# Add + RMSNorm streamed over one core: residual loads moved from SyncE's DMA queue to ScalarE's

## Chip, cores, metric

One core of a Trainium2 chip runs the kernel. The metric is the device time of one execution in microseconds (us).

## The reference

```python
x, residual: [32, 2048, 2048] float32;  gamma: [2048] float32;  eps = 1e-6
z = x + residual
rms = np.sqrt(np.mean(z ** 2, axis=-1, keepdims=True) + eps)
return (z / rms * gamma).astype(np.float32)
```

65536 rows of 8 KB. Two tensors are read and one is written, 1610.6 MB in all, with three or four simple operations per element.

## The kernel before

Rows go through SBUF (the on-chip memory) in tiles of 7 rows per partition: 128 partitions x 56 KB = 7168 KB per transfer. The first two tiles have 3 and 5 rows. Per tile there are three transfers (x in, residual in, z out) and this compute:

- VectorE adds the residual to z in place, in two parts, "a" of 3 rows and "b" of 4 rows.
- ScalarE squares each row with a running sum, part a then part b, and takes the root of each part.
- VectorE takes the reciprocals and scales each row by it and by gamma.

There are two z buffers, and one residual area of 11 rows for tiles of 7, so that the next residual tile may be loaded once part a of the add has freed its rows. SyncE issues every transfer, in this order (shortened, comments added):

```python
    def load_r(sp, t, d=0):
        i = t.i + d
        e = entry(i)
        inc(
            sp.dma_start(out=r_area[:, e : e + sizes[i], :], in_=rows(r_f, i)),
            "r_in",
            i,
        )

    def sp_turn(sp, t):
        i = t.i
        t.wait(sp, "done", -1)              # tile i-1 is scaled
        inc(sp.dma_start(out=rows(o_f, i - 1), in_=z[(i - 1) % 2][...]), "s_out", i - 1)
        if i == last:
            return
        t.wait(sp, "add_a")                 # part a of tile i is added: rows free
        load_r(sp, t, 1)
        t.wait(sp, "s_out", -1)             # store of tile i-1 has landed: z buffer free
        # ... last tile: x in four parts ...
        load_x(sp, t, 1)
```

ScalarE's turn for one tile (a `chain.wait` between its own instructions keeps their order):

```python
    def act_turn(s, t, chain):
        i, p = t.i, t.p
        for h, (a, b) in enumerate(parts(i)):
            chain.wait()
            t.wait(s, "add_a" if h == 0 else "add_b")
            inc(
                act_part(s, chain, z[p], a, b, ssq[p][h], rms[p][h][:, : b - a]),
                "rms_a" if h == 0 else "rms_b",
                i,
            )
```

## Time and profile before

| | before |
|---|---|
| time, median of 3 runs | 3726.41 us (3726.31 to 3726.53) |
| bytes moved, rate on the plateau | 1610.7 MB, 434 GB/s |
| share of the 16 DMA engines that is busy | 99.9% |
| VectorE, ScalarE busy | 62%, 29% |
| one tile | 50.77 us |

The lines behind this table are shown in the prediction. How to read them: in the queue lines the last number is the time that the queue's packets took as a share of 16 engines over the whole span; in the issue lines the last number is the median time from the issue to the landing, waiting in the queue included; in the instructions in order of time, the bracket is the time for which the engine sat idle and what ended it. As in the prediction, T is the moment at which VectorE starts to add a tile, which is when its x has landed.

### The profile page before, as it was taken

The numbers are of one execution on the slowest core, as the hardware profiler recorded it, in microseconds if no ns is written. First come the engines' busy times: TensorE is split into PE (matmuls) and PEld (weight loads), VectorE is DVE, ScalarE is ACT, GpSimd is POOL, SyncE is SP. The second block draws the span as 40 slices with busy tenths as digits, with TensorE's granted clock in tenths as the row PEclk, the third lists the DMA queues.
The fourth block names the chain that finished last, engine by engine and source line by source line (L and its number), as shares of the span: only waits on it lengthen the run. The fifth ranks groups of instructions, "written<-read, shape, count | busy, mean of one in ns | idle before, by whom it ended". The sixth has DMA issues, their size and how long they took to land.

```text
span 3724.5 us, 3677 instructions
## 1 busy us (share of the span) xinstructions
DVE 2302.6 (62%) x816; ACT 1072.4 (29%) x1176; POOL 0.2 (0%) x4
## 2 busy tenths in 40 slices
DVE  5666665566665566665566665566665566655566
ACT  2233322233322233322233322233322233322233
POOL 0000000000000000000000000000000000000000
DMA  9999999999999999999999999999999999999999
GB/s 421 431 434 434 433 434 436 434 434 434 434 434 434 434 434 434 434 434 434 434 434 434 434 434 434 434 434 434 434 434 434 434 434 434 434 434 434 434 433 399
DMA packets 32964, 1610.69 MB, mean 432 GB/s; under 512 B 3712, under 2 KB 3776, under 8 KB 3776
## 3 DMA queue, kind: packets, MB, share of 16 engines
q1 hardware_dynamic: 32960, 1610.66, 99.9%
q14 instruction: 4, 0.03, 0.0%
HBM read 1073.77 MB, written 536.87 MB: 432 GB/s over the span
## 4 chain that ended last, share of the span: by engine, by line
DMA 66%; DVE 22%; issue 10%; ACT 1%; SPq 0%; DVEq 0%; ACTq 0%
DMA out_dram<-z 33%; DMA z<-in_x_dram 33%; DVE z L170 15%; DVE z L175 7%; ACT sq_junk L221 1%; DMA r_area<-in_gamma_dram 0%; ACT rms L229 0%; DVE rstd L195 0%; DVEq L126 0%; SPq L255 0%; DVE r_area L271 0%; ACTq L209 0%; ACTq L126 0%; DVE tail_rstd L288 0%; SPq L160 0%
## 5 line engine op out<-in xcount | busy, mean ns | idle before, releaser
L170 DVE TENSOR_TENSOR z<-z,r_area 128x8192 f32<-128x8192 f32 (+2 forms) x150 | 1109.5, 7437 | 1253.0 <-DMA z<-in_x_dram 1226.8
L221 ACT ACTIVATE sq_junk<-z 128x2048 f32<-128x2048 f32 x512 | 963.4, 1882 | 2617.9 <-DVE z L170 2606.5
L175 DVE SCALAR_TENSOR_TENSOR z<-z,rstd,gamma_tile 128x2048 f32<-128x2048 f32 x505 | 1153.5, 2344 | 5.2
L195 DVE RECIPROCAL rstd<-rms 128x4 f32<-128x4 f32 (+2 forms) x146 | 25.3, 174 | 130.8 <-ACT rms L229 130.8
L221 ACT ACTIVATION_READ_ACCUMULATOR sq_junk<-z 128x1 f32 x512 | 95.4, 186 | 0.0
L229 ACT ACTIVATE rms<-ssq,eps_tile 128x4 f32<-128x4 f32 (+2 forms) x146 | 43.3, 297 | 13.4
L175 DVE SCALAR_TENSOR_TENSOR z<-z,tail_rstd,gamma_tile 128x2048 f32<-128x2048 f32 x7 | 16.2, 2346 | 0.1
L273 DVE LOAD_MASK_SELECT gamma_tile<-r_area x1 | 0.0, 14 | 16.4 <-DMA r_area<-in_gamma_dram 16.4
L273 DVE STREAM_SHUFFLE gamma_tile<-r_area 128x2048 f32<-128x2048 f32 x1 | 2.3, 2290 | 0.0
L271 DVE MEMSET r_area<- 128x2048 f32 x1 | 1.8, 1765 | 0.4 <-issue 0.4
L221 ACT ACT_TABLE_LOAD x1 | 1.3, 1283 | 0.9 <-SPq L75 0.9
L229 ACT ACT_TABLE_LOAD x1 | 1.3, 1283 | 0.1
L229 ACT ACTIVATE tail_rms<-tail_ssq,eps_tile 128x2 f32<-128x2 f32 (+1 forms) x4 | 1.2, 295 | 0.1
L270 DVE MEMSET eps_tile<- 128x1 f32 x1 | 0.1, 59 | 1.0 <-SPq L75 1.0
L288 DVE RECIPROCAL tail_rstd<-tail_rms 128x2 f32<-128x2 f32 (+1 forms) x4 | 0.6, 158 | 0.0
L345 POOL MEMSET const-bfloat16-1.0<- 128x1 bf16 x1 | 0.1, 102 | 0.0
L345 POOL MEMSET const-uint8-127<- 128x1 uint8 x1 | 0.1, 102 | 0.0
L345 POOL MEMSET const-float32-1.0<- 128x1 f32 x1 | 0.1, 99 | 0.0
L345 POOL MEMSET const-float32-0.0<- 128x1 f32 x1 | 0.1, 98 | 0.2 <-issue 0.2
## 6 DMA issues: line engine op xcount, KB each, us to landing
r_area<-in_residual_dram SPq DMA_DIRECT2D x72, 7168.0 KB, 27.2
z<-in_x_dram SPq DMA_DIRECT2D x71, 7168.0 KB, 33.8
out_dram<-z SPq DMA_DIRECT2D x71, 7168.0 KB, 34.4
z<-in_x_dram SPq DMA_DIRECT2D x3, 2048.0 KB, 26.3
out_dram<-z SPq DMA_DIRECT2D x3, 2048.0 KB, 14.1
r_area<-in_residual_dram SPq DMA_DIRECT2D x1, 5120.0 KB, 25.3
z<-in_x_dram SPq DMA_DIRECT2D x1, 5120.0 KB, 36.8
out_dram<-z SPq DMA_DIRECT2D x1, 5120.0 KB, 24.8
```

The source lines that it names most:

```text
L170: return v.tensor_add(out=s, in0=s, in1=r_area[:, e + a : e + b, :])
L175: ins = v.scalar_tensor_tensor(out=s, in0=s, scalar=rs[:, c + g - a : c + g - a + 1], in1=gamma_tile[:, :], op0=mult, op1=mult,)
L195: v.reciprocal(out=rstd[p][h][:, :n], in_=rms[p][h][:, :n]).then_inc(dve, U)
L221: s.activation(out=sq_junk[:, :], in_=src[:, g, :], func=Act.Square, accum_out=sq[:, g - a : g - a + 1],)
L229: return s.activation(out=rm, in_=sq[:, : b - a], func=Act.Sqrt, bias=eps_tile[:, :], scale=inv_d)
L270: v.memset(eps_tile[:, :], float(eps))
L271: v.memset(stage, 0.0).then_inc(tail_ev["add"], 1)
L273: v.stream_shuffle(gamma_tile[:, :].rearrange("p (a b) -> p a b", a=16), stage, [0] * 32)
L288: v.reciprocal(out=tail_rstd[:, a:b], in_=tail_rms[:, a:b]).then_inc(dve, U)
L345: nc = _bacc.Bacc("TRN2", target_bir_lowering=False, num_devices=1)
```

## The change

The intent: a residual load can be issued the moment its rows are free, by the engine that is waiting for that very event anyway, while SyncE keeps only the stores and the x loads. The core of the diff:

```diff
+    r_full = r_f[starts[2] :, :].rearrange("(n p r) m -> n p r m", p=P, r=R)
...
         inc(
-            sp.dma_start(out=r_area[:, e : e + sizes[i], :], in_=rows(r_f, i)),
+            sp.dma_start(
+                out=r_area[:, e : e + sizes[i], :],
+                in_=rows(r_f, i) if t.it is None else r_full[t.it + (i - 2)],
+            ),
...
         if i == last:
             return
-        t.wait(sp, "add_a")
-        load_r(sp, t, 1)
         t.wait(sp, "s_out", -1)
...
             t.wait(s, "add_a" if h == 0 else "add_b")
+            if h == 0 and i > 0:
+                load_r(s, t, 1)
             inc(
...
-        with s.Fori(0, 2 * n_iter, 2) as it:
+        with s.Fori(0, 2 * (n_iter - 1), 2) as it:
...
-        chain.n = n + 2 * R * n_iter
-        for i in range(HI, last):
+        chain.n = n + 2 * R * (n_iter - 1)
+        for i in range(HI - 2, last):
```

An unused semaphore (`fin`) goes as well. ScalarE's loop addresses the residual by its loop register, and its last iteration is peeled (written out after the loop).

More of the change, by code (lines that the diff above doesn't have):

```diff
@@ L96 @@
     s_tail = sem("s_tail")
-    fin = sem("fin")
     tail_ev = {k: sem(f"tail_{k}") for k in ("add", "rms", "done")}
```

## The prediction

> **What bounds the kernel now.** I read the head of the page and its DMA lines first, then the issues with their landing times, then one period of the instructions in order of time, then the waits of the issuing queue, then the two ends of the run. Head, slices and queues:
>
> ```profile
> span 3724.5 us, 3677 instructions
> DVE 2302.6 (62%) x816; ACT 1072.4 (29%) x1176; POOL 0.2 (0%) x4
> ...
> DMA  9999999999999999999999999999999999999999
> GB/s 421 431 434 434 433 434 436 434 434 434 434 434 434 434 434 434 434 434 434 434 434 434 434 434 434 434 434 434 434 434 434 434 434 434 434 434 434 434 433 399
> ...
> q1 hardware_dynamic: 32960, 1610.66, 99.9%
> ```
>
> One queue fills all 16 engines for 99.9% of the span. At the plateau of 434 GB/s its 1610.66 MB need 1610.66 / 0.434 = 3711 us; the span is 3724.5. So everything outside the plateau, both ends together, is about 13 us (0.35%). VectorE, the busiest compute engine, has 38% of the span free.
>
> ```profile
> r_area<-in_residual_dram SPq DMA_DIRECT2D x72, 7168.0 KB, 27.2
> z<-in_x_dram SPq DMA_DIRECT2D x71, 7168.0 KB, 33.8
> out_dram<-z SPq DMA_DIRECT2D x71, 7168.0 KB, 34.4
> ```
>
> A transfer of 7168 KB (7.34 MB) takes 7.34 / 0.434 = 16.9 us alone; every kind needs 27 to 34 us from issue to landing, so each waits 10 to 17 us behind another. Three of them make a tile: 3 x 16.9 = 50.8 us. One tile by the instructions in order of time (start, duration, engine, what):
>
> ```profile
> 1808.80 15.16 DVE L170 TENSOR_TENSOR z<-z,r_area 128x6144 f32<-128x6144 f32 x2 [17.58 <-DMA z<-in_x_dram]
> 1815.38 0.33 SPq L140 DMA_DIRECT2D r_area<-in_residual_dram  x1
> ...
> 1824.05 1.88 ACT L221 ACTIVATE sq_junk<-z 128x2048 f32<-128x2048 f32 x1 [2.20 <-DVE z L170]
> ...
> 1825.69 0.33 SPq L134 DMA_DIRECT2D z<-in_x_dram  x1
> ...
> 1842.01 0.34 SPq L149 DMA_DIRECT2D out_dram<-z  x1
> 1859.57 15.16 DVE L170 TENSOR_TENSOR z<-z,r_area 128x6144 f32<-128x6144 f32 x2 [17.59 <-DMA z<-in_x_dram]
> ```
>
> The period is 1859.57 - 1808.80 = 50.77 us, which is the three transfers and nothing else. Call 1808.8, when x of this tile is in, T. The store before has been in the queue since about T-17 and lands at T+16.9; the residual load is issued at T+6.6, the x load at T+16.9, the next store at T+33.2, each while an earlier transfer is still moving. The compute chain from x landed to the next store issued is 33.2 us of 50.8, so 17.6 us of it are slack: VectorE then idles (the 17.58) for the next x.
>
> ```profile
> SPq L140 <- DVE z L170: 1689.1, 72, 24.5
> SPq L149 <- DVE z L175: 1191.7, 73, 32.5
> SPq L134 <- DMA out_dram<-z: 697.1, 71, 10.0
> ```
>
> These are SyncE's waits as issuer. The first looks like the target: 1689.1 us behind the add before a residual load. But the add is what frees the rows; ScalarE waits for the same event. The store wait after it takes 697.1 / 71 = 9.8 us more, so the x load is never held by the add.
>
> [...] The trace agrees so far as it can: an issue is 0.33 us and lies beside a full pipe. [...] It does show that arrivals are in order of issue and that the steps from store to load to load cost nothing visible (50.77 against 3 x 16.9).
>
> **The change, part by part.**
>
> Removed: SyncE's wait for the add and its residual issue, for 72 tiles (tiles 0 and 1 stay on SyncE). That frees 72 x 0.33 = 24 us of SyncE, an engine that waits nearly always: 0 us on the path.
>
> Added: 72 issues on ScalarE, directly after the add that frees the rows and before the first square. The order of instructions shows, in the loop, one more register instruction ahead of each; VectorE's instructions are unchanged. At 0.33 to 0.6 us each (0.33 is SyncE's median, 0.58 its longest) this is 24 to 43 us of ScalarE. ScalarE's first group of squares ends and then it sits 2.20 us waiting for the second add (the bracket at 1824.05), so the issue is absorbed there and the second group starts when it did. On the path: 0 us. The loop loses one iteration of two tiles, which are peeled: same work.
>
> Moved: the moment of the residual issue does not move. Before, it is at T+6.6, right behind the add; after, the add's event lets ScalarE issue at T+6.6. What moves is its place. Before, it queues behind the store. After, it shares the engines with it. [...] The engines were never empty, so x lands when it does now[...]. The next store is issued at T+33.2, before x lands. The period stays 50.8.
>
> Ends: [...] the stores of the tile before still fill the engines until about 3706, and the last x part arrives when it did. Estimate 0 to 2 us. At the start the x load of tile 2 waits for the store of tile 0 (50.72) and not for the add (45.6), so nothing is won. Sum: 3726 + 0 to 2 us.
>
> **The rivals.** First, a bubble: x is issued only when the store before has wholly landed, and the store now lands late. If the residual gets more than its share, it may be through before x starts, and the engines stand idle for about 2 us per tile: 72 x 2 = 144 us, 3870 us (+4%). [...] For it: the 16 engines are not level (the DMA share in the last 18.5 us is only 0.63)[...].
>
> Second, a price of interleaving: store packets (SBUF to HBM) alternate with load packets of 56 KB. Per engine a transfer is 8 packets of 2.1 us; some 16 switches per tile. To cost 2%, a switch must cost 1.03 us / 16 = 64 ns. The queue of before changes direction twice per tile without a visible cost. [...]
>
> Third, a gain: mixed directions could run above the plateau. [...] a separate queue can otherwise win only the ends, 13 us: 3713 at the very best.
>
> Fourth, no interleaving at all: each engine finishes a transfer before it changes rows. Then the order is that of before, and the time too.
>
> **Range and chances.** The centre is the time before, 3726. Below it lie the ends (13 us, hardly reachable), above it the switch price and small bubbles. Range 3717 to 3742. Faster by over 2% would need 446 GB/s or more: 0.02. Slower by over 2% needs the bubble or 64 ns a switch: 0.05. Within 2%: 0.93.
>
> **What would show it.** A second hardware queue with about 72 x 7.34 = 528 MB, a third of the bytes, and the first with 1082 MB; together still 99% or more, slices at 434. Landing times: store 34.4 to about 43, x 33.8 to about 25, residual 27.2 to about 34; if they stay at 34, 34 and 27, there was no interleaving, and the time is right for another reason. SyncE's wait for the store should take over nearly all the 1689 us that it spent on the add. VectorE's wait for x stays near 17.6 us per tile, and the wait of the second reciprocal stays at 1.7. Wrong, and how: [...] DMA slices below 9 or a share near 96% mean the bubble; x landing before the residual, with VectorE waiting on the residual, means that the shares are not equal.

Passages are cut from the prediction at the marks. The cut sum under "Moved" assumed equal shares of an engine for two queues (later runs showed that their packets alternate one by one while both have work) and a start time of a load that no trace showed. It put the store's landing at T+25.7, the residual's at T+40.4 and x's at T+50.7, hence the period of 50.8 us; the landing times of 43, 25 and 34 us further down come from it. The "0 to 2 us" for the ends came from a first tail add that slips from 3677.2 to about 3679. The whole came to 3726 + 0 to 2 us, and the range of 3717 to 3742 also covered the cut allowance.

## The result, and the profile after

| | before | after |
|---|---|---|
| median of 4 runs | 3726.43 us | 3725.11 us |
| lowest to highest | 3726.31 to 3726.53 | 3724.70 to 3725.53 |

Ratio 0.9996, 95% interval 0.9979 to 1.0014: the same. (A ratio here is the mean time of one kernel's fast runs over the mean of the other's fast runs of the same rounds, so it need not equal the ratio of the medians.)

Head, slices and queues of the kernel after:

```profile
span 3723.7 us, 3798 instructions
...
GB/s 421 431 434 435 434 434 435 434 435 435 434 434 434 434 434 434 434 434 433 434 434 434 434 434 434 434 434 434 434 434 434 434 434 434 434 434 434 434 432 398
...
q1 hardware_dynamic: 22592, 1082.17, 67.2%
q10 hardware_dynamic: 10368, 528.49, 32.8%
```

The second queue carries the predicted 528 MB, the two together 100%, and the plateau stands at the same 434 GB/s. The issues, from the page's last part, show that the order did change:

```profile
r_area<-in_residual_dram ACTq DMA_DIRECT2D x72, 7168.0 KB, 35.5
z<-in_x_dram SPq DMA_DIRECT2D x71, 7168.0 KB, 27.5
out_dram<-z SPq DMA_DIRECT2D x71, 7168.0 KB, 40.8
```

The residual takes 8 us longer than before and the store 6 us longer, since they share the engines (packets of 2.116 us of the two queues alternate on an engine while both have work); the x load takes 6 us less, because it is issued later. One tile in order of time:

```profile
1807.81 15.16 DVE L172 TENSOR_TENSOR z<-z,r_area 128x6144 f32<-128x6144 f32 x2 [17.64 <-DMA z<-in_x_dram]
1814.55 0.34 ACTq L141 DMA_DIRECT2D r_area<-in_residual_dram  x1
...
1823.07 1.88 ACT L223 ACTIVATE sq_junk<-z 128x2048 f32<-128x2048 f32 x1 [1.67 <-DVE z L172]
...
1831.02 0.33 SPq L135 DMA_DIRECT2D z<-in_x_dram  x1
...
1841.03 0.34 SPq L153 DMA_DIRECT2D out_dram<-z  x1
1858.63 15.16 DVE L172 TENSOR_TENSOR z<-z,r_area 128x6144 f32<-128x6144 f32 x2 [17.63 <-DMA z<-in_x_dram]
```

The residual is still issued at T+6.7 and the next store at T+33.2. The x load is now issued at T+23.2, 6.3 us later than before, and yet the next tile starts 50.8 us after this one, as before. ScalarE's slack ahead of its second group went from 2.20 to 1.67 us: the issue was paid from there. SyncE's waits:

```profile
SPq L135 <- DMA out_dram<-z: 2828.4, 71, 43.0
SPq L153 <- DVE z L177: 735.1, 73, 32.2
```

Before, in the lines shown in the prediction, SyncE waited 1689.1 us for adds, 1191.7 for scaled tiles and 697.1 for stores, 3577.9 together; in these two lines it now waits 3563.5. A wait of 1689 us was removed from an engine, and it waits as long as it did.

### The profile page after: what moved, and what is told of

Its sections match the earlier page's. It is cut to its first block, busy times and chain, and to the rows that moved or that the text cites. A ratio compares the mean times of both kernels' runs of the same rounds, so it can differ in the third digit from the quotient of the medians.

```text
span 3723.7 us, 3798 instructions
## 1 busy us (share of the span) xinstructions
DVE 2302.6 (62%) x816; ACT 1072.4 (29%) x1176; POOL 0.2 (0%) x4
## 4 chain that ended last, share of the span: by engine, by line
DMA 67%; DVE 22%; issue 9%; ACT 2%; SPq 0%; DVEq 0%; ACTq 0%
DMA out_dram<-z 39%; DMA z<-in_x_dram 27%; DVE z L172 15%; DVE z L177 7%; ACT sq_junk L223 1%; ACT rms L231 0%; DVE rstd L197 0%; SPq L259 0%; DVEq L127 0%; DVE r_area L275 0%; ACTq L211 0%; ACTq L127 0%; SPq L141 0%; DVE tail_rstd L292 0%; SPq L162 0%
## 6 DMA issues: line engine op xcount, KB each, us to landing
r_area<-in_residual_dram ACTq DMA_DIRECT2D x72, 7168.0 KB, 35.5
z<-in_x_dram SPq DMA_DIRECT2D x71, 7168.0 KB, 27.5
out_dram<-z SPq DMA_DIRECT2D x71, 7168.0 KB, 40.8
```

## The experiments

All results are correct to the reference.

For some readings I summed the packet records of the traces myself. In these records each of the 16 engines moves a transfer of 7168 KB as 8 packets of 56 KB, followed by a packet of 4 bytes. "Long" is said of a packet that takes clearly more than the usual 2.116 us. The profile's views do not print such sums, so the tables of them are in ordinary fences. Columns of the first: the mean period of a tile; the mean time of one 56 KB packet on either queue (the median is 2.116 us in every run); the share of packets over 2.2 us on either; and the time per tile and engine in which no packet ran, which is the period minus 24 packets (16 of them on SyncE's queue where there are two queues, all 24 where there is one).

```
run          period   packet us          over 2.2 us      idle, us
             us       SyncE   ScalarE    SyncE  ScalarE   per tile
before       50.80    2.118   -          0.1%   -          0.0
after        50.80    2.118   2.117      0.0%   0.1%       0.0
x_first      54.55    2.193   -          8.3%   -          1.9
late_r_mid   52.44    2.185   2.182      6.7%   10.6%      0.0
late_r_end   54.61    2.158   2.268      6.1%   13.6%      1.9
late_r_sq1   50.81    2.118   2.117      0.2%   0.1%       0.0
late_r_sq2   50.86    2.120   2.122      1.1%   2.0%       0.0
dve_1        50.80    2.118   2.117      0.1%   0.1%       0.0
dve_2        51.80    2.140   2.184      3.1%   10.1%      0.1
```

The theory: the engines are kept full by both kernels, and while they are, the order of packets does not matter. The rivals: a small real gain or price of the second queue (a price per switch), or a compute chain that carries part of the time.

**after_again: the changed kernel, five rounds.** No edit.

> The changed kernel once more, for a narrower interval. Theory (the engines are always full, only the order of packets changes): 3725 us, ratio to before between 0.999 and 1.001. Rival (a small real gain or price of the second queue): a ratio that stays away from 1 by over 0.1% in every round.

Measured: 3724.97 us median, 3724.78 to 3725.36, against 3726.38; ratio 0.9996 (0.9983 to 1.001). No run of before lies below 3726.0 and none of after above 3725.6, so some 1.4 us (0.04%) may well be real, but the interval includes 1. I did not find its place for certain: in the two profiles the kernel after is already 0.3 us ahead at the first add, before any changed instruction has run. It stays open.

**x_first: the kernel before, x ahead of the residual on the one queue.**

```diff
-        t.wait(sp, "add_a")
-        load_r(sp, t, 1)
         t.wait(sp, "s_out", -1)
         load_x(sp, t, 1)
+        t.wait(sp, "add_a")
+        load_r(sp, t, 1)
```

> The kernel before, all on SyncE's queue, with the x load ahead of the residual load (it still waits for the store before; the residual load still waits for its rows). The bytes are the same. Theory: what keeps the engines full while the store's landing is reported and the x load starts up is the residual transfer in the pipe; without it there is one empty gap of 1.5 to 2 us per tile, 72 x 1.5 to 2 = 108 to 144 us, so 3830 to 3870 us; the DMA rate falls from 434 to about 418 to 422 GB/s. Rival (order never matters, as the bytes alone set the time): 3726 us within 8.

Measured: 4000.99 us, ratio 1.0739 (1.0722 to 1.0755). The queue line and one tile:

```profile
q1 hardware_dynamic: 32960, 1610.66, 96.4%
```

```profile
1939.79 15.16 DVE L170 TENSOR_TENSOR z<-z,r_area 128x6144 f32<-128x6144 f32 x2 [21.38 <-DMA r_area<-in_residual_dram]
...
1956.60 0.33 SPq L134 DMA_DIRECT2D z<-in_x_dram  x1
1956.97 0.43 SPq L140 DMA_DIRECT2D r_area<-in_residual_dram  x1
```

The store lands at T+16.8, the x load is issued then, and nothing else is in the pipe. So order does matter where it lets the pipe run dry: the rival that bytes alone set the time is out. The gap was foreseen (1.9 us per tile in the table, 1.5 to 2 expected), but the price is twice that: 54.55 - 50.80 = 3.75 us. The other 1.8 us are in packets that take longer than 2.116 us. In each tile they come in two sets, one per engine each time: the first x packet after the gap, at T+17.8, takes about 2.8 us, and the last residual packet before the next store, at T+50.3, about 3.3 us (means of the tiles in the middle of the run).

**late_r_mid: the changed kernel, residual issued after the first group of squares.**

```diff
             t.wait(s, "add_a" if h == 0 else "add_b")
-            if h == 0 and i > 0:
-                load_r(s, t, 1)
             inc(act_part(...), "rms_a" if h == 0 else "rms_b", i)
+            if h == 0 and i > 0:
+                load_r(s, t, 1)
```

> The changed kernel with the residual load issued on ScalarE after the first group of squares, about 6.5 us later (T+13.2 in place of T+6.7, T being when x is in). Theory: it is still issued before the store would land by itself at T+16.9, so the engines stay full: 3725 us within 8. Landing times move towards: residual about 31, x about 31, store about 37 us. Rival (the early issue is what the changed kernel lives on, or ScalarE's issue delays the squares): slower by 0.5% or more.

Measured: 3847.26 us, ratio 1.0329 (1.0313 to 1.0345). I had expected no change: this is the one clear miss. The queues and a tile by the windows (period, busy times, clock, DMA share, GB/s):

```profile
q1 hardware_dynamic: 22592, 1082.17, 67.0%
q10 hardware_dynamic: 10368, 528.49, 32.7%
```

```profile
1921.45 15.16 DVE L172 TENSOR_TENSOR z<-z,r_area 128x6144 f32<-128x6144 f32 x2 [19.01 <-DMA z<-in_x_dram]
1934.36 0.34 ACTq L141 DMA_DIRECT2D r_area<-in_residual_dram  x1
...
1940.37 0.33 SPq L135 DMA_DIRECT2D z<-in_x_dram  x1
```

```profile
1921.45:1973.75 52.30, 31.42 (x12) 14.61 (x16) 0.00 (x0) 1.00 1.00 421
```

The engines are busy for 99.7% and move only 421 GB/s: the busy share shows no loss, and the rate does. The loss sits in long packets: the first residual packets at T+13.9 to T+14.5 on 12 of the 16 engines (in a tile from the middle of the run), and again one packet per engine around T+46. Those 12 engines had just finished the store. I had reckoned with the store's landing at T+16.9, but that is the slowest engine. In the kernel before, the 16 parts of one transfer land over 4.0 us (median; in a transfer from the middle 10 engines lie within 0.4 us, and the last five come 2.6 to 4.0 us after the first), so the first part of the store lands at about T+12.9. In late_r_mid it lands at T+14.2 (median), 1.3 us after the residual is issued.

The engines hardly stand idle over this: 0.07 us per tile and engine, at T+13 to T+15. The time is in the packets, and how long the first residual packet on an engine takes goes with how soon after the issue it starts:

```
starts, us after the issue    0.9-1.1  1.1-1.3  1.3-1.5  1.5-1.8  1.8-2.4  2.4-2.8  2.8-3.2  3.2-3.6
us above 2.116, mean          0.80     0.70     0.55     0.39     0.29     0.28     0.11     0.02
```

The first x packets of x_first, on engines that did stand idle, give the same: 0.84 us more at 0.9 to 1.0 us after the issue, 0.54 at 1.2 to 1.5. So this set goes with the lead, the time from the issue to the moment when an engine gets to the load (below about 3 us the first packet is long), and not with whether the engine is empty. The set around T+46 is not explained by this, since those packets had been queued for long.

**late_r_end: the same after both groups.**

```diff
+            if h == 1 and i > 0:
+                load_r(s, t, 1)
```

> The changed kernel with the residual load issued on ScalarE after both groups of squares, at about T+24. Theory: the store then lands at T+16.9 with nothing else in the pipe, so each tile has a gap of at least 1.5 to 2 us, and the late residual shares with the x load and with the next store and lands after x: at least 3830 us, probably 3850 to 4050, and VectorE waits for the residual in place of x. Rival (the moment of the issue does not matter while the bytes are the same): 3725 us.

Measured: 4019.76 us, ratio 1.079 (1.0773 to 1.0806), inside the range. (The residual is issued at T+23.6.) The wait of VectorE turned over to the residual, as expected:

```profile
DVE z L172 <- DMA r_area<-in_residual_dram: 1547.1, 72, 26.4
```

The table shows the two parts again, 1.9 us of idle engines and 1.8 us of long packets per tile (54.61 - 50.80 = 3.81, rounded parts). "As soon as its rows are free" is thus worth 7.9% in the kernel after; but the kernel before had that issue time already.

**late_r_sq1 and late_r_sq2: between the changed kernel and late_r_mid.** The issue follows the first, or the second, square of the first group.

```diff
             for g in range(a, b):
                 ... square of row g ...
+                if then is not None and g - a + 1 == min(N, b - a):   # N = 1 or 2
+                    then()                                              # load_r(s, t, 1)
```

> The changed kernel with the residual load issued on ScalarE after the first square, about 2.1 us later than in the changed kernel (T+8.8). Theory, corrected after the run with 6.2 us of delay cost 122 us: the 16 engines are up to 4 us apart, the leading ones finish the store at about T+12.9, and the residual's first packet comes about 1 us after its issue; so nothing runs dry: 3725 us within 8. Rival (the loss grows evenly with the delay, 122 us per 6.2 us): about 3766 us.

> The same with the issue after the second square, about 4.1 us later (T+10.9). Theory: first packet at about T+12, just ahead of the leading engines' end of the store at T+12.9: 3725 to 3760 us, and hardly any packet longer than 2.2 us. Rival (even growth): about 3806 us.

Measured: 3724.99 us (ratio 0.9996) and 3727.12 us (1.0001, interval 0.9984 to 1.0018; 3725.85 to 3730.72). The first says nothing: its issue is no later than in the kernel after (1915.93 - 1909.18 = T+6.75), because ScalarE issues the transfer while the square is still running:

```profile
1909.18 15.16 DVE L172 TENSOR_TENSOR z<-z,r_area 128x6144 f32<-128x6144 f32 x2 [17.64 <-DMA z<-in_x_dram]
1915.77 1.88 ACT L223 ACTIVATE sq_junk<-z 128x2048 f32<-128x2048 f32 x1 [33.67 <-DVE z L172]
1915.93 0.34 ACTq L141 DMA_DIRECT2D r_area<-in_residual_dram  x1
```

The second is at T+8.8, two and not four us later:

```profile
1913.69 15.16 DVE L172 TENSOR_TENSOR z<-z,r_area 128x6144 f32<-128x6144 f32 x2 [17.57 <-DMA z<-in_x_dram]
1922.47 0.34 ACTq L141 DMA_DIRECT2D r_area<-in_residual_dram  x1
```

An even growth of the loss (122 us for 6.2 us of delay) would make 40 us of these 2.0 us of delay; measured are 2 against the kernel after. So the loss does not grow evenly: it sets in steeply between T+8.8 and T+12.9. That fits the lead of about 3 us: in late_r_sq2 the first part of the store lands at T+11.9 (median), 3.1 us after the residual is issued, and 1 to 2% of the packets are already long.

**before_8k and after_8k: seven times as many packets.** Rows dealt to the partitions so that a partition's rows are not contiguous in DRAM, in both kernels.

```diff
-        return t[starts[i] : starts[i] + P * k, :].rearrange("(p r) m -> p r m", r=k)
+        return t[starts[i] : starts[i] + P * k, :].rearrange("(r p) m -> p r m", r=k)
```

> The kernel before with rows dealt to partitions so that a partition's rows lie 128 rows apart in DRAM: each packet becomes 8 KB in place of 56 KB, seven times as many, same bytes and result. It is the base for the next run; its own time is open, 3726 to 3900 us.

> The changed kernel with the same 8 KB packets, so about 112 changes of queue per tile and engine in place of 16. Theory (a change of queue costs nothing): the same as the run with 8 KB packets on one queue, within 0.5%; and with finer packets the landing times come nearer to the equal-share sum of the prediction, store 43, x 25, residual 34 us, if the difference of the changed kernel from it (40.8, 27.5, 35.5) comes from whole 2.1 us packets. Rival (a switch costs 20 ns or more): slower than its base by 112 x 0.02 = 2.2 us per tile, 4% or more.

Measured: 3798.37 us (1.0193 of before; 1.0176 to 1.021, "unclear" against a bound of 2%) and 3791.67 us (1.0175). Two queues are 0.18% faster than one here (3791.67 / 3798.37 = 0.9982). In before_8k a tile takes 51.80 us (one in the middle, 1895.99 to 1947.79), and its 22.02 MB make 425 GB/s in place of 434; the order of addresses changed with the packets, so their size alone is not shown to be the cause. The number of changes of queue was not the expected 112. Joining each packet record to the one that ends as it begins, I count about 54 per tile and engine, and about 7 in the kernel after (not 16): while both queues have work they alternate packet by packet, and for the rest of the tile one queue has the engine alone. The rival of a price per switch is still out: 20 ns would have cost 54 x 0.02 = 1.1 us per tile, 2%. After:

```profile
r_area<-in_residual_dram ACTq DMA_DIRECT2D x72, 7168.0 KB, 34.7
z<-in_x_dram SPq DMA_DIRECT2D x71, 7168.0 KB, 28.2
out_dram<-z SPq DMA_DIRECT2D x71, 7168.0 KB, 41.9
```

Against 35.5, 27.5 and 40.8 with large packets, the residual and the store moved only a little towards the 34 and 43 of the prediction, and the x load away from its 25. So whole packets are not the main reason for that difference. By the packet records, the first residual packet in the kernel after starts 3.9 us after its issue and every engine has one by 5.6 us; with 8 KB packets 3.5 to 3.9 us. On engines with nothing to do it was 0.95 us, which is 0.62 us after the end of the issue (the x load of x_first).

**dve_1 and dve_2: a longer compute chain in the kernel after.** One or two sums over four rows before the scaling, result unused.

```diff
             v.wait_ge(dve, own(i, h))
+            for j, _ in enumerate((4,) if h == 0 and i > 1 else ()):      # dve_2: (4, 4)
+                v.reduce_sum(out=junk[:, 2*p+j : 2*p+j+1], in_=z[p][:, <rows of part b>, :] ..., axis=X)
```

> The changed kernel with one more VectorE operation per tile between the adds and the scaling, a sum over four rows (8192 elements, about 8.6 us as the add of that size), result unused. It also covers the 1.7 us wait for the second root, so the store is issued about 7 us later, at T+40. Theory (the compute chain is hidden while the store is queued before the engines run out of x): 3725 us within 8, VectorE's wait for x down from 17.6 to about 10.7 us per tile. Rival (the chain carries part of the time): up to 72 x 7 = 500 us more.

> The same with two such sums, about 17.2 us, so the store is issued at about T+48.7, 2 us before x is in at T+50.7. Theory with the spread of the engines (the leading ones are through with x up to 4 us earlier, at about T+46.8, and a first packet comes 1 us after its issue): part of the engines run dry each tile, and packets around it get longer: 1 to 3 us per tile, 3790 to 3940 us. Rival (only the slowest engine counts; the slack of 17.6 us still covers it): 3725 us within 8.

Measured: 3724.78 us (0.9996) and 3803.35 us, ratio 1.0209 (1.0192 to 1.0226: slower, though "unclear" against a bound of 2%). In dve_1, VectorE does 604 us more and nothing happens:

```profile
DVE 2906.1 (78%) x887; ACT 1072.2 (29%) x1176; POOL 0.2 (0%) x4
```

```profile
DVE z L173 <- DMA z<-in_x_dram: 769.8, 72, 12.6
```

The compute chain is hidden, and its wait for x gave the time. In dve_2 (two instructions of its timeline):

```profile
1896.75 15.16 DVE L173 TENSOR_TENSOR z<-z,r_area 128x6144 f32<-128x6144 f32 x2 [2.25 <-issue]
...
1945.35 0.34 SPq L154 DMA_DIRECT2D out_dram<-z  x1
1949.19 15.16 DVE L173 TENSOR_TENSOR z<-z,r_area 128x6144 f32<-128x6144 f32 x2 [3.87 <-issue]
```

The store is issued at T+48.6. VectorE still waits 3.87 us for x after that, so by the slowest engine the chain is still hidden; the run is 2.1% slower. The range was taken from late_r_mid, and the time came out in it, but not all as I had thought. The parts of the x load land over 1.4 us here and not over 4 (the first at T+50.2, 1.6 us after the store is issued), and the engines stand idle for 0.14 us per tile, at T+48 to T+50. The first packets of the store are not long (0.03 us at most in the mean). The long packets come later, in about every other tile: store packets at T+9.3 and the first residual packets at T+12. They follow the idle time: after a tile with 0.02 us of it or more, the packets of the next tile took 1.4 us per engine too long in all, otherwise 0.4 us. Why they come there stays open.

**x_once: x ahead of the residual in tile 36 alone, in the kernel before.** The edit is that of x_first under `if i == 36`.

> The kernel before with x ahead of the residual in tile 36 alone. In the run that does it in every tile each tile lost 3.75 us: about 1.95 with empty engines and 1.8 in packets longer than 2.12 us. Theory (each dry spell costs this once, and the full queue then heals it): about 4 us in this tile, under 1 us in each later tile; 3730 to 3736 us, and no long packets some ten tiles on. Rival (running dry puts the engines into a state that stays): every later tile loses about 1.8 us, 36 x 1.8 = 65 us, 3790 us.

Measured: 3730.43 us against 3726.47, 4.0 us. By slices:

```profile
GB/s 420 431 434 436 434 434 434 434 433 433 433 433 433 433 433 434 435 435 436 400 436 435 432 435 434 434 432 434 433 433 433 433 433 434 436 434 434 434 434 408
```

One slice falls to 400 and the next is back. By the packet records, time above 2.116 us per packet, mean of the 16 engines, in us for the tile and the ten after it:

```
1.89 0.04 0.04 0.04 0.07 0.11 0.07 0.13 0.11 0.08 0.03
```

So a dry spell is paid once, with the long packets in its own tile; it doesn't leave the engines in a slow state. After it the engines are in step again (in the next five tiles the parts of a transfer land within 0.4 to 1.0 us), and packets are not long. Being in step is thus not what makes them long. What makes the last load packet before the next store long after a dry spell, as at T+50.3 in x_first and T+46 in late_r_mid, stays open.

## Why the prediction was right, and where its steps were not

- **The bound.** Right. 434 GB/s and a period of 50.8 us in both kernels; dve_1 shows that the compute chain is not in the sum.
- **Removed: 0 us.** Right, and for the reason given: SyncE's wait moved to the store (697.1 to 2828.4 us).
- **Added on ScalarE: 0 us.** Right. 0.34 us per issue, 72 times, out of ScalarE's slack; the second reciprocal still waits 1.70 us.
- **Moved: x lands when it did.** Right in its result, wrong in one term of the sum. It took a time from the issue to the first byte that no trace showed: each transfer of that size in the trace of before waits in the queue. On engines at work it was 3.9 to 5.6 us in the kernel after, longer than I had put, so fewer of the store's packets had to share. In a middle tile of the kernel after, 12 engines are through with the store at T+17.0 to T+17.8 and the slowest at T+22.7, where the store's last two packets and its packet of 4 bytes each came behind a residual packet. The x load is issued 0.5 us after that, at T+23.2 in place of my T+25.7. The error cancels: whatever share the store loses, x gets back.
- **Ends: 0 to 2 us.** The first tail add did not slip: 3676.4 against 3677.2 before. In the last tile SyncE's four x issues took 7.16 us together, against 1.75 before; it cost nothing here, and its cause stays open.
- **Rival one, the bubble.** Rightly rejected: nothing runs dry in the kernel after (0.0 us of idle engines per tile). But two statements were wrong. A bubble costs 3.75 us per tile and not about 2 (x_first: 1.9 idle, 1.8 in long packets). And I had taken one on the leading engines to cost nothing but their lead: late_r_mid lost 3.3% and dve_2 2.1% with engines idle for only 0.07 and 0.14 us per tile. I had not reckoned with this cost, and the range held because the residual is issued early enough: at T+6.7, where T+8.8 cost about 2 us in all and T+12.9 cost 122.
- **Rival two, the switch price.** The price is 0 as far as the runs can tell (two queues against one: 0.9996 with 56 KB packets, 0.9982 with 8 KB). A full pipe at a low rate, which I had taken for its mark, came without it: late_r_mid ran at 421 GB/s in the shown tile, and its engines were busy for 99.7% of the run; its packets were long. The "some 16 switches per tile" were about 7.
- **Rival three, a gain.** None clear of noise with 56 KB packets: at most the 1.4 us above. With 8 KB packets two queues gained 0.18% (6.7 us), and its cause stays open.
- **Rival four, no interleaving.** Out: all three landing times moved.
- **Chances.** The "446 GB/s or more" for a gain of 2% is a slip: 1610.66 MB in 0.98 x 3726 - 13 us need about 443.

In sum, issuing from a second engine saved issue time on SyncE (72 x 0.33 = 24 us) and, with 56 KB packets, nothing else that is clear of noise (ratio 0.9996).

## What to carry to other kernels

With the DMA engines full, as here (99.9% busy), moving a transfer to another queue changed who waits and for how long, not the time (ratio 0.9996); look first whether the wait that you remove is one that anything waits for. What did count is that a load is issued in time for the leading one of the 16 engines, not the slowest: a lead of 1.3 us cost 3.3% (late_r_mid), one of 3.1 us next to nothing (late_r_sq2). The landing in the profile is that of the slowest engine: in the kernel before, the parts of one transfer land over 4.0 us (median). And judge a full pipe by its GB/s beside its busy share, since long packets count as busy: 421 GB/s at 99.7% in late_r_mid, 434 at 99.9% in the kernel before.
